# Mixture-of-experts block on one Trainium2 core: routing on tokens before their norm, and where the constants around it are prepared

## The chip, the cores and the metric

The kernel runs on one core of a Trainium2 chip. The metric is device time of one execution in microseconds (us), lower is better. A core has TensorE (PE: matrix products and transposes, in the order of its queue), VectorE (DVE), ScalarE (ACT), GpSimd (POOL), and SyncE (SP), which here only issues transfers. Each engine works through its own queue in order. An instruction that waits holds up all that stands behind it on its engine.

## The reference, cut to what matters

Two transformer blocks run one after the other. The change lies in the first, between the output projection of its mixers and its mixture of experts:

```python
x = layer_norm(DEEPNORM_ALPHA * x + mix @ w_out, ln1_g, ln1_b)   # 512 tokens x 1024
logits = x @ router_w + router_b                                 # 512 x 32 experts
top_val, top_idx = lax.top_k(logits, 4)
gate = softmax(top_val)
for e in range(32):                                              # rows = tokens that chose e
    hg, hl = split(x[rows] @ w_gu[e] + b_gu[e], 2)               # 1024 -> 2 x 1024
    hg, hl = min(hg, 7), clip(hl, -7, 7)
    y = ((hl + 1) * hg * sigmoid(1.702 * hg)) @ w_down[e] + b_down[e]
    ffn[rows] += gate * y
h = DEEPNORM_ALPHA * x + ffn
```

`layer_norm(x) = (x - mean) * rsqrt(var + 1e-5) * g + b`. All is float32. Since the experts' inputs depend on the top-4 choice, the logits are computed to float32 accuracy.

## The kernel before, in words

All of what follows is `block1_ffn` (from L1153). It handles the 512 tokens as 4 tiles of 128 (`NCH`), and three stretches of it matter here.

**Projection and router (393 to 470 us).** For each tile, two halves of 512 columns are projected into PSUM (bank `gu`). A product to float32 accuracy takes three matmuls with operands split in a high and a low part (`mm3`, L1148 to L1150), so a half is 24 matmuls. DVE adds the residual (L1283). `row_norm` takes statistics (DVE L1096, L1097, L1083), then a reciprocal root by Ln and Exp on ACT (L1084, L1085, each with its own table load), then normalises with two passes of 1024 columns on DVE (L1103, L1104). The normed tile is written to DRAM (`x1_d`, L1286; tiles 0 to 2 from POOL, tile 3 from SP). ACT makes a scaled copy (L1288), and POOL writes it to `h_d` (L1289), to which the experts' outputs are added later. PE transposes the normed tile in two halves of four (L1297), ACT copies each half out of PSUM (L1298), and 8 float32 matmuls against `rw` give the logits (L1301). DVE adds the bias (L1303), takes the top 4 and their softmax (L1311 to L1324).

After the last tile, small matmuls count each expert's tokens (L1331 to L1334), DVE forms ranks (L1335, L1336) and bfloat16 parts of the gates (`aux`, L1344 to L1348), and `slots` turns them into token lists: a comparison (L1408), four matmuls (L1411), and the index vector `ix` (L1419). POOL's indirect transfer gathers the first expert's 96 rows from `x1_d` with `ix` (L1428), and PE transposes them (L1230). **This gather is where the experts begin.**

**Constants, prepared beside the projection.** SP loads x, gains, biases and the expert bias `b_gu`. `bias` holds `b_gu` in three bfloat16 parts in three groups of 32 partitions: ACT rounds (L1260), and DVE takes differences and rounds them again, three subtractions and three casts of 32x2048 (L1265, L1266). The matmul L1443 adds that bias in the expert loop. The down bias `bdn` is loaded on ACT's queue and converted (L1354 to L1356).

**Experts (478 to 1690 us).** Each of 32 experts is 12 weight units of 1 MB. ACT rounds a unit to its high part `wh` (L1213), DVE subtracts it to get the low part `wl` (L1214), PE multiplies (L1148 to L1150). The units lie in a ring of 6 raw buffers and 3 spare ones, and 4 buffers for each part. For the first expert, unit 0 is used unsplit (L1451), and units 1 to 4 are split in pieces of 512 columns while the projection still runs; the low parts of units 1 and 2 are POOL's (8 pieces), those of 3 and 4 DVE's (8 pieces).

The program is written tile by tile; a scheduler builds each engine's queue from it, with its own estimate of when each instruction is ready. So code written later can stand earlier in a queue.

Of the kernel before, what the change touches and what calls it, by code (L numbers as in the profile page):

```python
# [126 lines left out]
def layout(inp):  # L127
# [34 lines left out]
    for n, k in (("w0", "rwkv_w0"), ("a0", "rwkv_a0"), ("k_k", "rwkv_k_k"), ("k_a", "rwkv_k_a"),  # L162
# [183 lines left out]
def bcast(ap_dram, off, n, parts=128):  # L346
    return bass.AP(tensor=ap_dram.tensor, offset=ap_dram.offset + off, ap=[[0, parts], [1, n]])
# [805 lines left out]
def block1_ffn(k, mix, wo, es_mix, b2):  # L1153
# [5 lines left out]
    with es:  # L1159
# [29 lines left out]
        def raw(n=2048, rows=128, p=ring, bufs=N_RAW):  # L1189
            return p.tile([128, 2048], F32, name="w", tag="w", bufs=bufs)[:rows, :n]  # L1190
# [47 lines left out]
        with tile_pool(tc, name="w1", bufs=1) as w1:  # L1238
# [9 lines left out]
            strict = w1.tile([128, 128], F32, name="strict")  # L1248
            nc.sync.dma_start(ident, A["cst"][:, 0:128])
            nc.sync.dma_start(strict, A["cst"][:, 128:256])  # L1250
            nc.sync.dma_start(cst2, A["cst"][:, CF["iota"][0]:CF["iota"][0] + 129])
            nc.sync.dma_start(rw, A["router_w"])
            nc.sync.dma_start(rb, bcast(A["router_b"], 0, 32))


            braw = raw(rows=96)
            for i in range(3):
                nc.sync.dma_start(braw[32 * i:32 * i + 32], A["b_gu"])
# [9 lines left out]
            ob_ = w1.tile([128, 128], BF, name="onesb")  # L1268
            V.tensor_copy(sb_, strict)
            G.memset(ob_, 1.0)  # L1270
            eye3 = sm.tile([128, 32], F32, name="eye3")
            V.tensor_add(eye3, ident[:, 0:32], ident[:, 32:64])
            V.tensor_add(eye3, eye3, ident[:, 64:96])
            M = w1.tile([128, NCH, N_EXP], F32, name="M")
            Mb = w1.tile([128, NCH, N_EXP], BF, name="Mb")
            for t in range(NCH):
                c = slice(128 * t, 128 * t + 128)
                for n in range(2):
# [58 lines left out]
            V.tensor_copy(cnt, p[:, NCH])  # L1337

            gr = w1.tile([128, NCH, N_EXP], F32, name="gr")
            V.tensor_copy(aux[:, :, :, 0].rearrange("p t e -> p (t e)"), pidx.to_broadcast([128, NCH * N_EXP]))  # L1340
            for t in range(NCH):
                G.memset(aux[:, t, :, 1], float(t))
            G.memset(aux[:, :, :, 2], 1.0)
            V.tensor_copy(aux[:, :, :, 3], Gm)  # L1344
            V.tensor_sub(gr, Gm, aux[:, :, :, 3])
            V.tensor_copy(aux[:, :, :, 4], gr)
            V.tensor_sub(gr, gr, aux[:, :, :, 4])
            V.tensor_copy(aux[:, :, :, 5], gr)  # L1348
            V.tensor_scalar(dslot, pidx, float(S), None, op0=OP.add)
# [45 lines left out]
        with tile_pool(tc, name="ex", bufs=1) as ex:  # L1395
# [106 lines left out]
            def expert_unit(e, i):  # L1502
# [1048 lines left out]
```

## Time and profile before

| | |
|---|---|
| median of 3 runs | 3124.77 us (3122.93 to 3128.39) |
| the profiled execution's own time | 3125.81 us |
| its span in the trace | 3124.0 us |
| mean granted TensorE clock | 0.964 of full speed |
| busy share over the span | PE 95%, DVE 65%, ACT 48%, POOL 17% |

The shares are averages over very different stages. The windows say what an engine does in one stretch, the timelines give the order within it, and "idle before <-releaser" says how long an engine waited and what ended the wait.

### The profile page before, as it was taken

The page shows a single profiled execution, that of the slowest core. Times are in us where ns is not written, and L with a number is a line of the kernel's source. Part 1 is how long each engine was busy: PE and PEld are TensorE (multiplying, and loading weights), DVE is VectorE, ACT ScalarE, POOL GpSimd, SP SyncE. Part 2 cuts the span into 40 slices and gives each one's busy share as a digit, 9 for nine tenths or more (in the row PEclk, how much of TensorE's full clock was granted, in tenths as well). Part 3 has the DMA queues.
Part 4 walks back from the last instruction along what each step waited for, and adds up shares of the span by engine and source line. Part 5 has one row for each costly group of instructions (what it writes and reads, how often), then busy time and mean ns, then how long its engine had stood idle before and what let it go on. Part 6 is the DMA issues. An engine that isn't in the chain of part 4 may idle for free. (4 is left out here: it accounts for less than half of the span.)

```text
span 3124.0 us, 41785 instructions
## 1 busy us (share of the span) xinstructions
PE 2966.2 (95%) x16609; PEld 2386.3 (76%) x16609; DVE 2037.0 (65%) x2862; ACT 1491.3 (48%) x1855; POOL 537.4 (17%) x444
## 2 busy tenths in 40 slices
PE   6899888999999999999999999999999899999997
PEld 4799765666666666666666888999999799888886
DVE  4755767988888888788887756654233846733324
ACT  4412346666666666666665633342222534432222
POOL 1210231101210000121002210320102501320104
PEclk8989989999999999999999989999999989999998
DMA  3201177989999999799996211122222211222221
GB/s 124 75 21 41 61 268 289 357 341 366 366 358 359 361 359 353 290 388 356 360 355 229 73 67 43 55 82 95 95 82 82 93 45 55 82 95 95 95 90 52
DMA packets 106263, 581.87 MB, mean 186 GB/s; under 512 B 13080, under 2 KB 13736, under 8 KB 56048
## 3 DMA queue, kind: packets, MB, share of 16 engines
q1 hardware_dynamic: 95120, 542.17, 44.9%
q0 software_dynamic: 10752, 36.47, 4.8%
q8 instruction: 132, 2.16, 0.3%
q10 hardware_dynamic: 192, 0.52, 0.1%
q14 instruction: 67, 0.55, 0.1%
HBM read 560.17 MB, written 18.94 MB: 185 GB/s over the span
## 5 line engine op out<-in xcount | busy, mean ns | idle before, releaser
L1214 DVE TENSOR_TENSOR wl<-w,wh 128x2048 fp32r<-128x2048 f32 (+1 forms) x367 | 800.8, 2197 | 125.7 <-ACT wh L1213 121.4
L1213 ACT ACTIVATE wh<-w 128x2048 fp32r<-128x2048 f32 (+1 forms) x375 | 668.3, 1810 | 51.4 <-PE gu L1150 34.9
L1816 PE MATMUL gu<-hh,w 128*128 128x264 f32 (+3 forms) x1336 | 419.0, 314 | 10.0 <-ACT hh L2518 10.0
L1817 PE MATMUL gu<-hl,w 128*128 128x264 f32 (+3 forms) x1336 | 415.6, 311 | 3.9 <-DVE hl L2520 3.8
L1818 PE MATMUL gu<-hh,w 128*128 128x264 f32 (+3 forms) x1336 | 413.5, 310 | 0.8 <-DVE w L1142 0.8
L1142 DVE TENSOR_TENSOR w<-w 128x1024 fp32r<-128x1024 f32 (+1 forms) x190 | 237.5, 1250 | 249.2 <-ACT w L1141 248.7
L1148 PE MATMUL gu<-wh,xT 128*96 128x512 f32 x896 | 371.9, 415 | 0.0
L1149 PE MATMUL gu<-wl,xT 128*96 128x512 f32 x896 | 359.4, 401 | 7.4 <-DVE wl L1214 7.2
L1150 PE MATMUL gu<-wh,xT 128*96 128x512 f32 x896 | 351.4, 392 | 0.0
L1141 ACT ACTIVATE w<-w 128x1024 fp32r<-128x1024 f32 (+1 forms) x194 | 201.3, 1038 | 297.7 <-PE gu L2338 89.6
L1816 PEld LDWEIGHTS gu<-hh,w 128*128 128x128 f32 x1336 | 260.0, 195 | 22.4 <-ACT hh L2518 11.6
L1817 PEld LDWEIGHTS gu<-hl,w 128*128 128x128 f32 x1336 | 260.0, 195 | 16.1 <-DVE hl L2520 5.0
L1818 PEld LDWEIGHTS gu<-hh,w 128*128 128x128 f32 x1336 | 260.5, 195 | 11.2 <-DVE w L1142 1.3
L1149 PE MATMUL py<-wl,hT 128*96 128x512 f32 x512 | 211.7, 413 | 1.8 <-DVE wl L1214 0.4
L1149 PEld LDWEIGHTS gu<-wl,xT 128*96 128x96 f32 x896 | 144.1, 161 | 87.1 <-DVE wl L1214 23.2
L1148 PE MATMUL py<-wh,hT 128*96 128x512 f32 x512 | 208.8, 408 | 1.4 <-ACT wh L1213 1.4
L1150 PE MATMUL py<-wh,hT 128*96 128x512 f32 x512 | 202.8, 399 | 0.0
L1148 PEld LDWEIGHTS gu<-wh,xT 128*96 128x96 f32 x896 | 144.4, 161 | 67.3 <-issue 7.4
L1150 PEld LDWEIGHTS gu<-wh,xT 128*96 128x96 f32 x896 | 145.4, 162 | 58.5
L2324 POOL TENSOR_TENSOR al<-fs,ah 128x528 fp32r<-128x528 f32 (+1 forms) x44 | 77.7, 1767 | 595.0 <-ACT ah L2323 595.0
L1428 POOL DMA_INDIRECT xg<-x_d,ix x32 | 72.8, 2275 | 505.5 <-DVE dx L1421 439.4
L1481 POOL DMA_INDIRECT h_d<-y,dx x31 | 60.6, 1955 | 526.2 <-ACT y L1480 496.6
(714 smaller groups left out, 6133.4 us busy)
## 6 DMA issues: line engine op xcount, KB each, us to landing
w<-in_wgu SPq DMA_DIRECT2D x256, 1024.0 KB, 8.4
w<-in_wdn SPq DMA_DIRECT2D x127, 1024.0 KB, 8.3
w<-in_w SPq DMA_DIRECT2D x88, 512.0 KB, 4.2
w<-in_w2f SPq DMA_DIRECT2D x43, 512.0 KB, 4.2
w<-in_w22a SPq DMA_DIRECT2D x32, 512.0 KB, 4.1
w<-in_w1f SPq DMA_DIRECT2D x18, 512.0 KB, 3.3
w<-in_w2o SPq DMA_DIRECT2D x16, 512.0 KB, 4.2
w<-in_w22b SPq DMA_DIRECT2D x16, 384.0 KB, 3.9
```

Of the source, the lines that this page charges most:

```text
L1141: nc.scalar.activation(h, w, AF.Copy)
L1142: (eng or nc.vector).tensor_sub(l, w, h.bitcast(F32))
L1148: PE.matmul(out, a[0], b[0], start=start, stop=False)
L1149: PE.matmul(out, a[0], b[1], start=False, stop=False)
L1150: PE.matmul(out, a[1], b[0], start=False, stop=stop)
L1213: ACT.activation(h[:, j], w[:, j], AF.Copy)
L1214: (early or V).tensor_sub(l[:, j], w[:, j], h[:, j].bitcast(F32))
L1428: gathers.append(G.indirect_dma_start(out=xg, out_offset=None, in_=x1_d, in_offset=bass.IndirectOffsetOnAxis(ap=ix[:, :1], axis=0)))
L1816: PE.matmul(p, w[0][:, kk], x[0][:, kk, c], start=kk == ks[0], stop=False)
L1817: PE.matmul(p, w[0][:, kk], x[1][:, kk, c], start=False, stop=False)
L1818: PE.matmul(p, w[1][:, kk], x[0][:, kk, c], start=False, stop=kk == ks[-1])
L2324: G.tensor_sub(a[1], ss[f], a[0].bitcast(F32))
```

## The change: what it does

1. Layer norm's gain is multiplied into the router's weights, and the logits are taken from tokens that are not yet normed: `logit = rs * (x @ (g*W) - mean * sum(g*W)) + (b @ W + router_b)`. The two sums over the weights come from 8 + 8 float32 matmuls with a matrix of ones, ahead of the first projection's end. The norm passes on DVE no longer stand ahead of the transposes.
2. The projection of tile t+1 is written ahead of the router of tile t.
3. The three-part expert bias is prepared by POOL (one +1 pass, a memset, two subtractions of 64 and 32 partitions x 2048) and ACT (three roundings), DVE no longer takes part. `b_gu` is loaded four times, not three.
4. All 16 low-part pieces of the first expert go to DVE; POOL did 8.
5. The gates' bfloat16 parts are taken per tile.
6. The down bias is loaded and converted in expert 2, in a raw buffer of the ring.
7. The scaled copy for `h_d` is made in place after `x1_d` has been written, and its code stands after the first gather's.
8. SP's loads are in another order: first tile, router and bias constants, gains, then tiles 1 to 3.

```diff
-            for t in range(NCH):
-                nc.sync.dma_start(x[:, t], A["x"][128 * t:128 * t + 128])
+            nc.sync.dma_start(x[:, 0], A["x"][0:128])
...
+            for t in range(1, NCH):
+                nc.sync.dma_start(x[:, t], A["x"][128 * t:128 * t + 128])
-            V.tensor_scalar(braw[:, 1024:], braw[:, 1024:], 1.0, None, op0=OP.add)
-            ACT.activation(bias[0:96], braw, AF.Copy)
-            G.memset(bias[96:128], 0.0)
-            for i in range(1, 3):
-                b_, w_ = bias[32 * i:32 * i + 32], braw[32 * i:32 * i + 32]
-                for _ in range(i):
-                    V.tensor_sub(w_, w_, b_)
-                    V.tensor_copy(b_, w_)
+            G.tensor_scalar(braw[:, 1024:], braw[:, 1024:], 1.0, None, op0=OP.add)
+            ACT.activation(bias, braw, AF.Copy)
+            G.memset(bias[32:64], 0.0)
+            for a in (64, 96):
+                G.tensor_sub(braw[a:128], braw[a:128], bias[a:128])
+                ACT.activation(bias[a:128], braw[a:128], AF.Copy)
...
+            V.tensor_mul(rwb, rw, gb[:, 1, :, None].to_broadcast([128, 8, 32]))
+            for j in range(8):
+                PE.matmul(p[:, 0], ones, rwb[:, j], start=j == 0, stop=j == 7)
+            V.tensor_add(rb, rb, p[:, 0])
+            V.tensor_mul(rw, rw, gb[:, 0, :, None].to_broadcast([128, 8, 32]))
+            for j in range(8):
+                PE.matmul(p[:, 1], ones, rw[:, j], start=j == 0, stop=j == 7)
+            V.tensor_scalar(nsg, p[:, 1], -1.0, None, op0=OP.mult)
...
+            def project(t):
...
                     V.scalar_tensor_tensor(xs, xs, ALPHA1, p, op0=OP.mult, op1=OP.add)
-                xt = x[:, t]
-                row_norm(k, w1, xt, xt, g1, b1, fast=True)
-                x1w = (nc.sync if t == NCH - 1 else nc.gpsimd).dma_start(x1_d[c], xt)
-                xa = w1.tile([128, 8, 128], F32, name="x1T", bufs=2).rearrange("p a b -> p (a b)")
-                ACT.activation(xa, xt, AF.Copy, scale=ALPHA1)
-                nc.gpsimd.dma_start(h_d[c], xa)
...
+                    V.bn_stats(st[:, n], xs)
+                V.bn_aggr(mv, st.rearrange("p a b -> p (a b)"))
+                return mv
+            mvs = [project(0)]
+            for t in range(NCH):
+                if t + 1 < NCH:
+                    mvs.append(project(t + 1))
...
                     ACT.activation(xT[:, 4 * n:4 * n + 4], p, AF.Copy)
+                fast_rsqrt(k, w1, mv[:, 1:2], rs, eps=1e-5)
                 p = bank("py", (128, N_EXP))
                 for j in range(8):
                     PE.matmul(p, xT[:, j], rw[:, j], start=j == 0, stop=j == 7)
+                V.scalar_tensor_tensor(xt, xt, mv[:, 0:1], g1, op0=OP.subtract, op1=OP.mult)
+                V.scalar_tensor_tensor(xt, xt, rs, b1, op0=OP.mult, op1=OP.add)
+                x1w = (nc.sync if t == NCH - 1 else nc.gpsimd).dma_start(x1_d[c], xt)
-                V.tensor_add(lg, p, rb)
+                V.scalar_tensor_tensor(lg, nsg, mv[:, 0:1], p, op0=OP.mult, op1=OP.add)
+                V.scalar_tensor_tensor(lg, lg, rs, rb, op0=OP.mult, op1=OP.add)
...
+                V.tensor_copy(aux[:, t, :, 3], Gm[:, t])
+                V.tensor_sub(gr[:, t], Gm[:, t], aux[:, t, :, 3])
...
-            V.tensor_copy(aux[:, :, :, 3], Gm)
-            V.tensor_sub(gr, Gm, aux[:, :, :, 3])
...
         def gates():
+            bd = raw(D)
             for i in range(4):
                 nc.scalar.dma_start(bd[32 * i:32 * i + 32], A["b_dn"])
             ACT.activation(bdn, bd, AF.Copy)
             V.tensor_sub(bdn[64:128], bd[64:128], bdn[64:128].bitcast(F32))
...
-                    return unit(src, early=(G if i < 3 else V if i < 5 else None) if e == 0 else None)
+                    return unit(src, early=V if e == 0 and i < 5 else None)
...
             st = rows(*sl[0])
+            for t in range(NCH):
+                ACT.activation(x[:, t], x[:, t], AF.Copy, scale=ALPHA1)
+                nc.gpsimd.dma_start(h_d[128 * t:128 * t + 128], x[:, t])
```

The new file has two lines more in its helpers and others further down, so its line numbers differ: `mm3` is L1150 to L1152, Ln and Exp L1086 and L1087, the low part L1216, the sums with ones L1285 and L1290, the residual L1311, the transposes L1326 and their copies L1327, the router's matmuls L1331, the norm passes L1332 and L1333, the `x1_d` write L1334, the bias parts L1264 to L1269, the scaled copy L1583 and its write L1584.

**ACT's queue, from tile 0's rsqrt to tile 1's transposed copies.** Before (tile 1):

```order
L1084 ACT_TABLE_LOAD
L1084 ACTIVATE rn_rs<-rn_rs 128x1
L1085 ACT_TABLE_LOAD
L1085 ACTIVATE rn_rs<-rn_rs 128x1
L1288 ACTIVATE x1T<-x 128x1024
L1298 ACTIVATE x1T<-tr 128x512
L1260 ACTIVATE bias<-w 96x2048
L1298 ACTIVATE x1T<-tr 128x512
```

Now (from tile 0's Exp to tile 1's copies):

```order
L1087 ACTIVATE rs<-rs 128x1
L1327 ACTIVATE x1T<-tr 128x512
L1265 ACTIVATE bias<-w 128x2048
L1327 ACTIVATE x1T<-tr 128x512
L1349 ACTIVATE gt<-gt 128x4
L1269 ACTIVATE bias<-w 64x2048
L1583 ACTIVATE x<-x 128x1024
L1269 ACTIVATE bias<-w 32x2048
L1086 ACT_TABLE_LOAD
L1086 ACTIVATE rs<-rs 128x1
L1087 ACT_TABLE_LOAD
L1087 ACTIVATE rs<-rs 128x1
L1327 ACTIVATE x1T<-tr 128x512 x2
```

The three roundings of the bias (`bias<-w`) now stand between tile 0's copies and tile 1's. Before, one stood there, between tile 1's copies, and DVE did the later two.

**POOL's queue over the same stretch.** Before, then now:

```order
L805 TENSOR_TENSOR wo_2851<-wraw,wo_2850 128x1024 x4
L1261 MEMSET bias 32x2048
L1270 MEMSET onesb 128x128
L1342 MEMSET aux 128x32 x4
L1343 MEMSET aux 128x128
L1397 MEMSET top 128x1
L1286 DMA x_d<-x 128x1024
L1289 DMA h_d<-x1T 128x1024
L1292 DMA h_d<-x 96x1024
```

```order
L807 TENSOR_TENSOR wo_2851<-wraw,wo_2850 128x1024 x4
L1274 MEMSET onesb 128x128
L1275 MEMSET ones 128x128
L1298 MEMSET aux 128x32 x4
L1299 MEMSET aux 128x128
L1424 MEMSET top 128x1
L1264 TENSOR_SCALAR w<-w 128x1024
L1266 MEMSET bias 32x2048
L1268 TENSOR_TENSOR w<-w,bias 64x2048
L1334 DMA x_d<-x 128x1024
L1268 TENSOR_TENSOR w<-w,bias 32x2048
L1584 DMA h_d<-x 128x1024
```

The +1 pass, the memset and both subtractions of the bias follow the setting-up of `aux`. The memset waits for ACT's first rounding, the second subtraction for ACT's second.

**PE's queue around tile 1's router, now** (`gu` is the projection, of tile 2 up to the first three rows and of tile 3 from the fifth on):

```order
L1150 MATMUL gu<-wo_2850,mix_2852 128x512
L1151 MATMUL gu<-wo_2851,mix_2852 128x512
L1152 MATMUL gu<-wo_2850,mix_2853 128x512
L1326 MATMUL tr<-fcst,x 128x128 x8
L1150 MATMUL gu<-wo_2848,mix_2852 128x512
L1331 MATMUL py<-rw,x1T 128x32 x4
L1151 MATMUL gu<-wo_2849,mix_2852 128x512
L1331 MATMUL py<-rw,x1T 128x32 x4
L1152 MATMUL gu<-wo_2848,mix_2853 128x512
```

Of tile 3's 48 matmuls one stands ahead of the router's first half, which needs ACT's copy `x1T`; the other 47 stand behind it.

**DVE's queue toward the index vector, now** (tile 3's last part; `wl` are first-expert pieces):

```order
L1216 TENSOR_TENSOR wl<-w,wh 128x512
L1358 TENSOR_REDUCE Gm<-oh 128x32
L1374 SCALAR_TENSOR_TENSOR Rm<-py,M 128x128
L1359 CAST aux<-Gm 128x32
L1376 COPY cnt<-py 128x32
L1360 TENSOR_TENSOR gr<-Gm,aux 128x32
L1375 TENSOR_SCALAR Rm<-Rm 128x128
L1361 CAST aux<-gr 128x32
L1216 TENSOR_TENSOR wl<-w,wh 128x512
L1362 TENSOR_TENSOR gr<-gr,aux 128x32
L1435 TENSOR_TENSOR o_3573<-fcst_2992,Rm 128x384
L1363 CAST aux<-gr 128x32
L1216 TENSOR_TENSOR wl<-w,wh 128x512
```

Before, no piece stood ahead of `ix`; now six do, these three and three earlier ones.

## Rows read from the trace of the kernel before

**Rows 1.** Groups of instructions, 478 to 1690 us (the experts): busy, mean ns | idle before, releasers.

```profile
L1213 ACT ACTIVATE wh<-w 128x2048 fp32r<-128x2048 f32 (+1 forms) x359 | 659.3, 1863 | 49.5 <-PE gu L1150 34.7 <-PE py L1150 6.0 <-ACT wh L1213 5.4
...
L1149 PE MATMUL gu<-wl,xT 128*96 128x512 f32 x896 | 359.4, 401 | 7.4 <-DVE wl L1214 7.2
```

**Rows 2.** Windows: us; busy (instructions) of PE, PEld, DVE, ACT, POOL; clock; DMA share; GB/s.

```profile
400.00:446.00 46.00, 45.42 (x224) 37.64 (x222) 31.62 (x65) 16.02 (x25) 8.31 (x16) 1.00 0.67 246
455.00:478.00 23.00, 7.26 (x47) 6.77 (x48) 19.64 (x52) 9.30 (x17) 10.33 (x8) 0.50 0.66 219
461.73:469.97 8.24, 1.08 (x11) 0.78 (x10) 6.86 (x32) 2.40 (x5) 0.00 (x0) 0.50 0.78 242
```

**Rows 3.** PE's timeline: start, duration, line, operation xcount [idle before <-releaser].

```profile
393.34 0.80 PE L1148 MATMUL gu<-wo,mix 128*128 128x512 f32 x1 [2.79 <-DVE mix L584]
...
398.57 0.40 PE L1148 MATMUL gu<-wo,mix 128*128 128x512 f32 x1
...
401.78 0.39 PE L1150 MATMUL gu<-wo,mix 128*128 128x512 f32 x1
...
413.35 1.03 PE L1297 MATMUL tr<-fcst,x 128*128 128x128 f32 x8
414.13 0.49 PE L1150 MATMUL gu<-wo,mix 128*128 128x512 f32 x1
...
414.93 0.97 PE L1301 MATMUL py<-rw,x1T 128*128 128x32 f32 x8
415.74 0.48 PE L1150 MATMUL gu<-wo,mix 128*128 128x512 f32 x1
...
425.66 1.07 PE L1297 MATMUL tr<-fcst,x 128*128 128x128 f32 x8 [0.57 <-DVE x L1104]
...
445.71 0.40 PE L1150 MATMUL gu<-wo,mix 128*128 128x512 f32 x1
...
477.20 1.51 PE L1230 MATMUL tr<-fcst,xg 96*128 96x96 f32 x8 [8.21 <-DMA xg<-x_d,ix]
```

**Rows 4.** DVE's timeline, 418 to 486 us.

```profile
420.60 0.69 DVE L1283 SCALAR_TENSOR_TENSOR x<-x,gu 128x512 f32<-128x512 f32 x1 [0.76 <-PE gu L1150]
...
437.66 2.28 DVE L1265 TENSOR_TENSOR w<-w,bias 32x2048 f32<-32x2048 f32 x1
...
445.96 1.28 DVE L1104 SCALAR_TENSOR_TENSOR x<-x,rn_rs,b 128x1024 f32<-128x1024 f32 x1
...
469.83 0.14 DVE L1419 CAST ix<-tk 96x1 int32<-96x1 f32 x1
...
470.02 2.48 DVE L1214 TENSOR_TENSOR wl<-w,wh 128x512 fp32r<-128x512 f32 x4
```

**Rows 5.** ACT's timeline, 418 to 456 us.

```profile
422.70 1.28 ACT L1085 ACT_TABLE_LOAD   x1
423.99 0.20 ACT L1085 ACTIVATE rn_rs<-rn_rs 128x1 f32<-128x1 f32 x1
...
426.58 0.58 ACT L1298 ACTIVATE x1T<-tr 128x512 f32<-128x512 f32 x1
427.05 1.90 ACT L1260 ACTIVATE bias<-w 96x2048 bf16<-96x2048 f32 x1
...
449.20 1.15 ACT L1213 ACTIVATE wh<-w 128x512 fp32r<-128x512 f32 x2
```

**Rows 6.** POOL's timeline, 390 to 480 us.

```profile
392.97 9.44 POOL L805 TENSOR_TENSOR wo<-wraw,wo 128x1024 fp32r<-128x1024 f32 x4 [35.92 <-ACT wo L804]
402.47 1.80 POOL L1261 MEMSET bias<- 32x2048 bf16 x1
...
449.18 10.67 POOL L1214 TENSOR_TENSOR wl<-w,wh 128x512 fp32r<-128x512 f32 x7
```

**Rows 7.** The `x1_d` writes from POOL (L1286): issue to landing.

```profile
DMA to landing us min/median/max: 2.9/7.1/8.6
```

**Rows 8.** The longest `h_d` write (L1292): issue to landing.

```profile
DMA to landing us min/median/max: 12.9/12.9/12.9
```

More of the change, by code (lines that the diff above doesn't have):

```diff
@@ L186, in layout @@
     o["router_w"] = np.ascontiguousarray(_pk(inp["router_w"][0]))
+    o["ln1c"] = np.ascontiguousarray(np.stack([inp[n][0].reshape(8, 128).T for n in ("ln1_g", "ln1_b")], 1))
     o["router_b"] = np.ascontiguousarray(inp["router_b"])
@@ L1243, in block1_ffn @@
             rb = w1.tile([128, 32], F32, name="rb")
-            for t in range(NCH):
-                nc.sync.dma_start(x[:, t], A["x"][128 * t:128 * t + 128])
+            gb = w1.tile([128, 2, 8], F32, name="gb")
+            nc.sync.dma_start(x[:, 0], A["x"][0:128])
+            strict = w1.tile([128, 128], F32, name="strict")
+            nc.sync.dma_start(ident, A["cst"][:, 0:128])
+            nc.sync.dma_start(rw, A["router_w"])
+            nc.sync.dma_start(gb, A["ln1c"])
+            nc.sync.dma_start(rb, bcast(A["router_b"], 0, 32))
@@ L1246, in block1_ffn @@
+            braw = raw(rows=128)
+            for i in range(4):
+                nc.sync.dma_start(braw[32 * i:32 * i + 32], A["b_gu"])
             nc.sync.dma_start(g1, bcast(A["rows2"], 0, D))
             nc.sync.dma_start(b1, bcast(A["rows2"], D, D))
-            strict = w1.tile([128, 128], F32, name="strict")
-            nc.sync.dma_start(ident, A["cst"][:, 0:128])
             nc.sync.dma_start(strict, A["cst"][:, 128:256])
             nc.sync.dma_start(cst2, A["cst"][:, CF["iota"][0]:CF["iota"][0] + 129])
-            nc.sync.dma_start(rw, A["router_w"])
@@ L1267, in block1_ffn @@
+            G.tensor_scalar(braw[:, 1024:], braw[:, 1024:], 1.0, None, op0=OP.add)
[4 more added lines that the diff above has]
+                ACT.activation(bias[a:128], braw[a:128], AF.Copy)
             sb_ = w1.tile([128, 128], BF, name="strictb")
             ob_ = w1.tile([128, 128], BF, name="onesb")
+            ones = w1.tile([128, 128], F32, name="ones")
@@ L1269, in block1_ffn @@
             V.tensor_copy(sb_, strict)
             G.memset(ob_, 1.0)
+            G.memset(ones, 1.0)
             eye3 = sm.tile([128, 32], F32, name="eye3")
-            V.tensor_add(eye3, ident[:, 0:32], ident[:, 32:64])
-            V.tensor_add(eye3, eye3, ident[:, 64:96])
+            V.tensor_add(eye3, ident[:, 0:32], ident[:, 64:96])
+            V.tensor_add(eye3, eye3, ident[:, 96:128])
+            rwb = w1.tile([128, 8, 128], F32, name="x1T", bufs=2)[:, :, 0:32]
+            V.tensor_mul(rwb, rw, gb[:, 1, :, None].to_broadcast([128, 8, 32]))
@@ L1274, in block1_ffn @@
             M = w1.tile([128, NCH, N_EXP], F32, name="M")
             Mb = w1.tile([128, NCH, N_EXP], BF, name="Mb")
+            gr = w1.tile([128, NCH, N_EXP], F32, name="gr")
+            V.tensor_copy(aux[:, :, :, 0].rearrange("p t e -> p (t e)"), pidx.to_broadcast([128, NCH * N_EXP]))
             for t in range(NCH):
+                G.memset(aux[:, t, :, 1], float(t))
+            G.memset(aux[:, :, :, 2], 1.0)
+            V.tensor_scalar(dslot, pidx, float(S), None, op0=OP.add)
+            def project(t):
@@ L1277, in block1_ffn @@
                 c = slice(128 * t, 128 * t + 128)
+                st = w1.tile([128, 2, 6], F32, name="st", bufs=2)
+                mv = w1.tile([128, 2], F32, name="mv", bufs=2)
                 for n in range(2):
@@ L1283, in block1_ffn @@
                     V.scalar_tensor_tensor(xs, xs, ALPHA1, p, op0=OP.mult, op1=OP.add)
-                xt = x[:, t]
-                row_norm(k, w1, xt, xt, g1, b1, fast=True)
-                x1w = (nc.sync if t == NCH - 1 else nc.gpsimd).dma_start(x1_d[c], xt)
-                xa = w1.tile([128, 8, 128], F32, name="x1T", bufs=2).rearrange("p a b -> p (a b)")
-                ACT.activation(xa, xt, AF.Copy, scale=ALPHA1)
-                nc.gpsimd.dma_start(h_d[c], xa)
-                if t == 0:
-                    nc.gpsimd.dma_start(h_d[S:], x[:NS, 0])
+                    V.bn_stats(st[:, n], xs)
[5 more added lines that the diff above has]
+                    mvs.append(project(t + 1))
+                c, xt, mv = slice(128 * t, 128 * t + 128), x[:, t], mvs[t]
+                rs = w1.tile([128, 1], F32, name="rs", bufs=2)
                 xT = w1.tile([128, 8, 128], F32, name="x1T", bufs=2)
-                for q in range(2):
+                for n in range(2):
                     p = bank("tr", (128, 4, 128))
                     for i in range(4):
-                        PE.transpose(p[:, i], xt[:, 512 * q + 128 * i:512 * q + 128 * i + 128], ident)
-                    ACT.activation(xT[:, 4 * q:4 * q + 4], p, AF.Copy)
+                        PE.transpose(p[:, i], xt[:, 512 * n + 128 * i:512 * n + 128 * i + 128], ident)
+                    ACT.activation(xT[:, 4 * n:4 * n + 4], p, AF.Copy)
+                fast_rsqrt(k, w1, mv[:, 1:2], rs, eps=1e-5)
                 p = bank("py", (128, N_EXP))
@@ L1337, in block1_ffn, with gates @@
             V.tensor_copy(cnt, p[:, NCH])
[L1339 to L1343, printed above, removed]
-            V.tensor_copy(aux[:, :, :, 3], Gm)
-            V.tensor_sub(gr, Gm, aux[:, :, :, 3])
[L1346 to L1349, printed above, removed]
             spare.append(es_b.enter_context(tile_pool(tc, name="spare2", bufs=1, side="right")))
             wb = es_b.enter_context(tile_pool(tc, name="wb", bufs=1, side="right"))
-            bd = w1.tile([128, 8, 128], F32, name="x1T", bufs=2).rearrange("p a b -> p (a b)")
+        def gates():
+            bd = raw(D)
             for i in range(4):
@@ L1553, in block1_ffn @@
             st = rows(*sl[0])
+            for t in range(NCH):
+                ACT.activation(x[:, t], x[:, t], AF.Copy, scale=ALPHA1)
+                nc.gpsimd.dma_start(h_d[128 * t:128 * t + 128], x[:, t])
+            nc.gpsimd.dma_start(h_d[S:], x[:NS, 0])
             sl.append(first(1))
```

10 lines of the change are left out of this document (5 added, 5 removed).

## The prediction

> **What bounds the kernel now.** I read four things in this order. First the groups of the experts' stretch: PE's low-part matmuls stood idle for 7.4 us in 1212 us, and ACT's splits waited mostly for PE [rows 1]. So PE sets the pace there, and a first gather that comes some us later moves the end by as much. Then the windows: from 400 to 446 us PE is busy 45.42 of 46.00 us at a granted clock of 1.00 (the 2.4 GHz level), while DVE, ACT and POOL have room; from 455 to 478 us PE is busy 7.26 of 23.00 at 0.50 (1.2 GHz) [rows 2]. So the projection is PE's, and after it comes a tail of small steps, most of them on DVE. Third PE's timeline, for prices and for the two fixed points: the last projection matmul starts at 445.71 and takes 0.23 until the next could start, so the projection ends at 445.94 [rows 3]. The index vector `ix` is ready at 469.83 + 0.14 = 469.97 [rows 4]. **The tail is 24.0 us.** Then PE waits for the gather [rows 3]. Last, the timelines of ACT and POOL, since the order of the changed program puts their bias work between two tiles.
>
> My sum is therefore the time of `ix` after the change against 469.97. All from there on is taken as shifted with it.
>
> **The projection, PE alone.** From 398.57 to 401.78 fourteen matmuls start, 0.229 each; elsewhere in the stretch 0.227, so I take 48 of a tile as 10.9 us [rows 3]. A tile's eight transposes hold the next start up by 0.78, and that matmul's successor by 0.10 more: 0.88. Half a router (4 steps, 8 passes) costs 0.81 + 0.10 = 0.91 the same way [rows 3]. The 16 float32 matmuls with ones have the shape of four such halves: 4 x 0.91 = 3.65, added to the projection. Two tiles' routers lay inside the projection before and do so now, so they cancel. The wait of 0.57 for the normed tile 1 goes, since transposes no longer need the norm [rows 3]. Without any new stall the projection would end at 445.94 + 3.65 - 0.57 = **449.0**.
>
> **The new stall.** ACT's queue now has the three bias roundings between tile 0's and tile 1's copies, and two of them wait for POOL's subtractions. In before, tile 1's second projected half reached DVE at 420.60, 0.1 after its end [rows 4]. Now tile 0's router (0.88 + 2 x 0.91 = 2.7) comes behind this point, and the ones (3.65) before it: 420.5 - 2.7 + 3.65 = 421.4. Four transposes and one copy (0.58) later, at 422.6, the chain starts:
> - ACT's first rounding, 1.90 by the one of before [rows 5]; POOL's memset behind it, 1.80 [rows 6];
> - subtraction, d; rounding 1.90; subtraction, d; rounding 1.90;
> - Ln and Exp of tile 1 with their table loads, 2 x (1.28 + 0.20) [rows 5]; the copy of half a tile, 0.58 [rows 5]; six hand-overs between engines, 0.1 each as in the 0.1 above.
>
> Without d that is 422.6 + 11.6 = 434.2. For d the trace has no row of this shape. POOL's four subtractions of 1024 columns took 9.44, so 2048 would take 4.7; its seven pieces of 512 beside a busy DVE took 10.67, so 2048 would take 6.1 [rows 6]. The number of partitions should not matter: on DVE 32 partitions x 2048 took 2.28 and four pieces of 128 x 512 took 2.48 [rows 4]. I take **d = 5.2**, nearer to the first, since DVE now has pauses; its lower bound is DVE's own 2.28. The chain ends at 444.6. PE is ready for tile 1's router after tile 2's projection (10.9), tile 0's transposes and router (2.7), tile 1's transposes (0.88) and one matmul (0.33): 421.4 + 14.8 = 436.2. **PE stands for 8.4 us**, with 47 matmuls of tile 3 behind it. The other engines' tile-3 work waits for those in turn.
>
> After the idle stretch at 393 us the first twelve matmuls took 5.23 (393.34 to 398.57) and not 2.7: the clock was at its lower level [rows 3]. I add 2.5 for the same after the stall; zero is the other bound. The projection then ends at 449.0 + 8.4 + 2.5 = **459.9**.
>
> POOL's rate itself: four passes of 1024 took 9.44, so 2.36 each, against half of 2.28 on DVE [rows 4, 6]. The Trainium skill, GPSIMD Engine Reference, section 3.1 on elementwise work, measures 4497 ns for a subtraction-like pass of 2048 float32 on GpSimd against 2293 ns on Vector and says to keep elementwise work on Vector; that speaks against this edit, and the trace agrees within 5% (4.7 for 2048). By its 4.5 for d the stall would be 7.0, and the sum below 1.4 us less.
>
> **The tail.** DVE has 62 operations from the last residual to `ix` in the new order. Two take 0.69 and four norm passes 1.28 [rows 4]: 6.5. Six are pieces of 0.62 (a quarter of 2.48) [rows 4]: 3.7; before, none stood ahead of `ix`. Fifty are small: 32 of their kind were busy 6.86 us [rows 2], less about 1.0 because five casts and differences of `aux` now have 32 columns and not 128, so 0.18 each: 9.2. Together 19.4. The last norm pass also waits for tile 3's Exp. By then ACT has done six pieces (0.57 each by 1.15 for two), four copies (0.53), two loads and two small steps, 8.5 [rows 5], and has waited some 1.8 for transposes at the lower clock, 10.3 in all. DVE is at that pass after 7.5, so it waits 2.8. Hand-overs 0.2. **Tail: 22.4**, 1.6 less than before: the norm left the way to the transposes, but the pieces came into it.
>
> `ix` is then ready at 459.9 + 22.4 = 482.3, 12.3 later. The profiled execution took 3125.81, which gives 3138.1. It is 1.04 above the median, so against the median the forecast is **3137.1 us**.
>
> **What I cost at nothing.** DVE's own bias work was under PE's projection, which never waited longer than the 0.57 for DVE [rows 2, 3]; taking it away gives nothing but that. POOL's +1 pass lies at 405 us, 17 us ahead of the chain; without that cover it would cost 2.4. The down bias in expert 2 takes one ring buffer and a wait of ACT under PE-bound work; 0 to 3 us. SP's new order lets weights start some 2 us later, all ahead of their use. The gates' parts are in the tail's count. The gather stands behind tile 3's `h_d` write on POOL, and that waits for tile 3's `x1_d` write to land and for ACT's scaling: 11.6 into the tail + 0.3 + 8.6 [rows 7] + 1.1 + 0.5 = 22.1, just under 22.4. With a landing of 12.9 [rows 8] it is 26.3, 3.9 late. These are the next two things to be late.
>
> **The rivals.** *Gather held by the write* (for it: the margin of 0.3; against: the median landing is 7.1 [rows 7]): 12.3 + 3.9 = +16.2, 3141.0; with d = 6.1 another 1.8, 3142.8. *POOL is quick, and the time stays* (the other side): the order alone causes no stall if each subtraction ends in time. PE stands 8.4 - 2 x (5.2 - d), so at DVE's 2.28 it stands 2.6, and no stall is left at d = 1.0. Then 449.0 + 22.4 gives +1.4, 3126.2. With 2.6 of stall but no loss of clock it is +4.0, 3128.8; it decides at d below about 2.1, where stall and clock together stay within +6.2. Against it: no POOL pass in the trace is that quick. *The tail is freed and the stall absent* (for it: pieces may fill waits that exist anyway, and matmuls with ones may run while PE waits for its weights): 445.4 + 15.9 (22.4 less 3.7 and 2.8) = 461.3, 8.7 earlier, 3116.1. Against it: PE was busy through the projection, and the pieces' places are fixed in DVE's queue. *The change not doing what it says* is excluded by the order.
>
> **How the numbers follow.** Stalled forecast 0.60 (with d from 4.7 to 6.1 and the tail's wait of 2.8 hidden or not: 3133 to 3139), gather held as well 0.12, no loss 0.18, gain 0.10. A measurement of this kernel can tell about 0.2%, 6.2 us, from no change. Slower by more is the first two, 0.72; same is the third and a fifth of the fourth, 0.20; faster 0.08. The range runs from 3126.0, the foot of the third, to 3143.0, the head of the second; it leaves out the fourth and an outlier above, under 0.2.
>
> **What would show it.** Right: PE idle some 8 us around 436 to 445 at the router's half of tile 1, released by ACT's copy; ACT there waiting twice for POOL's subtraction of about 5 us; a lower clock after it; `ix` near 482; no piece on POOL. Wrong: a POOL subtraction near 2 us; PE's projection unbroken until 449; or the gather released by something other than `ix`. If the experts' stretch from gather to end is longer or shorter by over 2 us, the shift does not pass to the end as taken.

## The result, and the profile after

The changed kernel takes 3143.38 us (median of 6 runs, 3134.23 to 3148.99) against 3123.85 (6 runs of before in the same sessions, 3112.45 to 3128.39). The ratio is 1.0072, with an interval from 1.0055 to 1.0090: **slower by 17 to 28 us**, where 12.3 was forecast. The profiled execution took 3148.99 us, span 3147.1, granted clock 0.962.

Totals scatter by up to 20 us (29 runs of before: 3110.6 to 3130.9), and part of that arises ahead of the stretch studied here: in the profiles the projection starts between 379.2 and 395.4 us, though the experiments' edits concern only what comes behind. So the mechanisms are read from stretches that begin at the projection's start. There kernels with the same order agree: the tail is 20.4 us in four of them (changed, e2, e3, f0), and the projection 53.2 or 53.3 in four of the five with the same three repairs, 54.1 in the fifth. From there to the end the kernel before took 2730.7 us (3124.0 - 393.3) and the changed one 2754.8 (3147.1 - 392.3): 24.1 more.

That starting point flatters the kernel before by 3.1 us. There PE waited 2.79 us for the last mixer's output before the projection [rows 3]; in the changed kernel, and in all its variants, the projection follows that mixer's matmuls with no wait, 1.60 us after their start and not 4.73. Counted from those matmuls (388.61 before, 390.73 after) the change costs 21.0 us. Which of its eight parts removed the wait was not tested.

```profile
388.61 1.94 PE L580 MATMUL ps<-cst,ml_h 128*128 128x128 f32 x8 [4.32 <-DVE ml_h L572]
```

| stretch, us | before | forecast | after |
|---|---|---|---|
| projection, first to last matmul | 52.6 | 66.6 | 75.1 |
| tail, to the index vector `ix` | 24.0 | 22.4 | 20.4 |
| `ix` to the transposes of the gathered rows | 7.2 | 7.2 | 10.4 |
| sum | 83.9 | 96.2 | 105.9 |

PE's timeline after the change, with the waits that answer to [rows 3]:

```profile
390.73 1.94 PE L582 MATMUL ps<-cst,ml_h 128*128 128x128 f32 x8 [4.32 <-DVE ml_h L574]
392.33 0.78 PE L1150 MATMUL gu<-wo,mix 128*128 128x512 f32 x1
...
404.60 0.50 PE L1151 MATMUL gu<-wo,mix 128*128 128x512 f32 x1 [0.68 <-POOL wo L807]
...
408.09 3.59 PE L1285 MATMUL py<-x1T,ones 128*128 128x32 f32 x16 [2.76 <-DVE x1T L1282]
411.49 0.77 PE L1150 MATMUL gu<-wo,mix 128*128 128x512 f32 x1
...
412.49 3.46 PE L1290 MATMUL py<-rw,ones 128*128 128x32 f32 x16
415.76 0.77 PE L1152 MATMUL gu<-wo,mix 128*128 128x512 f32 x1
...
451.23 1.92 PE L1331 MATMUL py<-rw,x1T 128*128 128x32 f32 x8 [6.49 <-ACT x1T L1327]
452.96 0.77 PE L1151 MATMUL gu<-wo,mix 128*128 128x512 f32 x1
...
467.44 1.03 PE L1326 MATMUL tr<-fcst,x 128*128 128x128 f32 x8
...
498.22 1.52 PE L1232 MATMUL tr<-fcst,xg 96*128 96x96 f32 x8 [11.41 <-DMA xg<-x_d,ix]
```

Two places broke the projection. The forecast one is there: PE waits 6.49 us for ACT's `x1T` at tile 1's router. The other is at the matmuls with ones (L1285, L1290): a wait of 2.76, then 3.40 and 3.27 us for what was costed at 1.8 each, and matmuls that start 0.43 apart, not 0.23. Two windows give the clock (the columns are those of [rows 2]); before, it was 1.00 from 400 to 446 us [rows 2]:

```profile
411.00:422.00 11.00, 11.00 (x38) 9.50 (x38) 2.12 (x6) 1.69 (x3) 0.00 (x0) 0.53 0.98 406
452.00:462.00 10.00, 10.00 (x38) 8.54 (x38) 4.93 (x21) 3.81 (x6) 1.07 (x2) 0.65 0.44 179
```

Who held PE at the ones stands in three queues, DVE's, ACT's and POOL's:

```profile
406.01 0.15 DVE L1426 TENSOR_SCALAR top<-top 128x1 f32<-128x1 f32 x1 [10.61 <-ACT top L1425]
406.10 0.69 DVE L1311 SCALAR_TENSOR_TENSOR x<-x,gu 128x512 f32<-128x512 f32 x1
...
407.53 0.42 DVE L1282 TENSOR_TENSOR x1T<-rw,gb 128x256 f32<-128x256 f32 x1
```

```profile
405.78 0.20 ACT L1425 ACTIVATE top<-top 128x1 f32<-128x1 f32 x1 [6.61 <-POOL top L1424]
```

```profile
402.18 2.37 POOL L807 TENSOR_TENSOR wo<-wraw,wo 128x1024 fp32r<-128x1024 f32 x1
...
405.42 0.31 POOL L1424 MEMSET top<- 128x1 f32 x1
```

The weights' product with the bias (L1282) stands in DVE's queue behind a step on the constant `top`. That step waits for ACT's sigmoid, the sigmoid for POOL's memset of `top`, and the memset stands behind POOL's last pass over the output weights (L807, to 404.5) and its setting-up of other constants. A constant that nobody needs before the experts held up PE.

The stall at tile 1, in ACT's and POOL's queues:

```profile
430.73 1.90 ACT L1265 ACTIVATE bias<-w 128x2048 bf16<-128x2048 f32 x1
...
439.40 0.21 ACT L1349 ACTIVATE gt<-gt 128x4 f32<-128x4 f32 x1 [6.28 <-DVE gt L1348]
439.63 1.91 ACT L1269 ACTIVATE bias<-w 64x2048 bf16<-64x2048 f32 x1
...
445.76 1.91 ACT L1269 ACTIVATE bias<-w 32x2048 bf16<-32x2048 f32 x1 [3.12 <-POOL w L1268]
447.68 1.28 ACT L1086 ACT_TABLE_LOAD   x1
...
450.60 1.06 ACT L1327 ACTIVATE x1T<-tr 128x512 f32<-128x512 f32 x2
```

```profile
432.69 1.80 POOL L1266 MEMSET bias<- 32x2048 bf16 x1 [24.41 <-ACT bias L1265]
434.56 4.10 POOL L1268 TENSOR_TENSOR w<-w,bias 64x2048 f32<-64x2048 f32 x1
...
441.63 4.09 POOL L1268 TENSOR_TENSOR w<-w,bias 32x2048 f32<-32x2048 f32 x1 [2.42 <-ACT bias L1269]
```

The chain runs as forecast, rounding, memset, subtraction, rounding, subtraction, rounding, two table loads, copy. Only d is 4.1, not 5.2. DVE beside it shows something that was not forecast:

```profile
435.25 3.46 DVE L1337 SCALAR_TENSOR_TENSOR lg<-lg,rs,rb 128x32 f32<-128x32 f32 x1
...
441.80 4.07 DVE L1353 TENSOR_TENSOR oh<-fcst,ixf 128x128 f32<-128x128 f32 x1
```

Two small steps take 3.46 and 4.07 us and end 0.05 and 0.15 us after POOL's two subtractions. The first of them enters the chain: ACT's second rounding stands behind the exponential of tile 0's gates (L1349), whose operand DVE makes after that step. So the rounding starts 0.97 us after POOL's subtraction has ended (438.66), where the forecast has 0.1.

### The profile page after: what moved, and what is told of

Same layout as the page of the kernel before. It is cut to its first block, busy times and chain, and to the rows that moved or that the text cites. A ratio compares the mean times of both kernels' runs of the same rounds, so it can differ in the third digit from the quotient of the medians.

```text
span 3147.1 us, 41865 instructions
## 1 busy us (share of the span) xinstructions
PE 2977.9 (95%) x16641; PEld 2395.5 (76%) x16641; DVE 2032.7 (65%) x2886; ACT 1494.3 (47%) x1857; POOL 543.5 (17%) x440
## 5 line engine op out<-in xcount | busy, mean ns | idle before, releaser
L1216 DVE TENSOR_TENSOR wl<-w,wh 128x2048 fp32r<-128x2048 f32 (+1 forms) x375 | 805.8, 2163 | 122.2 <-ACT wh L1215 119.8
L1150 PE MATMUL gu<-wh,xT 128*96 128x512 f32 x896 | 371.9, 415 | 0.0
L1152 PE MATMUL gu<-wh,xT 128*96 128x512 f32 x896 | 351.4, 392 | 0.0
L1150 PE MATMUL py<-wh,hT 128*96 128x512 f32 x512 | 209.9, 410 | 1.4 <-ACT wh L1215 1.4
L1151 PEld LDWEIGHTS gu<-wl,xT 128*96 128x96 f32 x896 | 144.1, 161 | 87.4 <-DVE wl L1216 23.4
L1152 PE MATMUL py<-wh,hT 128*96 128x512 f32 x512 | 203.7, 400 | 0.0
L1150 PEld LDWEIGHTS gu<-wh,xT 128*96 128x96 f32 x896 | 144.4, 161 | 67.6 <-issue 7.5
L1152 PEld LDWEIGHTS gu<-wh,xT 128*96 128x96 f32 x896 | 145.4, 162 | 58.4
```

The lines of the kernel that those rows point to most:

```text
L1150: PE.matmul(out, a[0], b[0], start=start, stop=False)
L1151: PE.matmul(out, a[0], b[1], start=False, stop=False)
L1152: PE.matmul(out, a[1], b[0], start=False, stop=stop)
L1216: (early or V).tensor_sub(l[:, j], w[:, j], h[:, j].bitcast(F32))
```

## The experiments

Theory S is the forecast's stall. Theory O came from the trace after: the sums with ones. The numbers in the table are us of the profiled execution, from the projection's start as above; the ratio is that of the whole times to before, with its 95% interval.

| kernel | projection | tail | `ix` to transposes | sum | ratio |
|---|---|---|---|---|---|
| before | 52.6 | 24.0 | 7.2 | 83.9 | 1 |
| changed | 75.1 | 20.4 | 10.4 | 105.9 | 1.0072 (1.0055 to 1.0090) |
| e1 | 63.5 | 28.3 | 10.2 | 102.0 | 1.0072 (1.0046 to 1.0098) |
| e2 | 68.6 | 20.4 | 9.9 | 98.9 | 1.0049 (1.0026 to 1.0071) |
| e12 | 57.2 | 28.4 | 10.7 | 96.3 | 1.0032 (1.0012 to 1.0051) |
| e3 | 65.1 | 20.4 | 10.5 | 95.9 | 1.0039 (1.0016 to 1.0062) |
| f0 | 59.0 | 20.4 | 10.0 | 89.4 | 1.0009 (0.9990 to 1.0028) |
| e23r | 53.2 | 22.1 | 10.9 | 86.2 | 1.0020 (1.0001 to 1.0039) |
| e23rg | 54.1 | 23.6 | 6.4 | 84.0 | 1.0026 (1.0008 to 1.0044) |
| e23rgb | 53.3 | 22.0 | 5.3 | 80.6 | 1.0019 (1.0003 to 1.0036) |
| f1 | 53.2 | 20.9 | 10.7 | 84.9 | 1.0005 (0.9989 to 1.0020) |
| f2 | 53.2 | 21.2 | 12.8 | 87.2 | 1.0011 (0.9995 to 1.0027) |
| gp | 73.5 | 23.4 | 9.9 | 106.7 | 1.0081 (1.0052 to 1.0110) |

**e1, the bias chain first.** ACT's copies for tile 0, its Ln and Exp for tiles 0 and 1 and the first scaled copy are ordered behind the last rounding, POOL's first `x1_d` write behind the last subtraction:

```diff
...
-                ACT.activation(bias[a:128], braw[a:128], AF.Copy)
+                rnd = ACT.activation(bias[a:128], braw[a:128], AF.Copy)
...
+                    with tc.issue_after(rnd.ins) if t == 0 else nullcontext():
                         ACT.activation(xT[:, 4 * n:4 * n + 4], p, AF.Copy)
+                with tc.issue_after(rnd.ins) if t < 2 else nullcontext():
                     fast_rsqrt(k, w1, mv[:, 1:2], rs, eps=1e-5)
...
```

> The changed kernel with one order edit: ACT's three roundings and POOL's two subtractions of the expert bias are held ahead of tile 0's transposed copies, Ln and Exp; nothing is computed otherwise. Theory S (the bias chain between tile 0's and tile 1's copies is most of the loss): the wait of 6.5 us of PE at tile 1's router is gone, and with it about 3.3 us at the lower clock, so the kernel gains 10 us on the changed one and stands about 10 us above before. Theory O (the sums with ones are most of the loss): the wait goes, but the time stays within 3 us of the changed kernel, since PE loses its clock at the ones anyway.

The stall was gone and the projection 11.7 us shorter, but the tail grew by 7.9, and the total did not move (ratio 1.0072 again). In ACT's queue tile 0's Exp now stood behind tile 1's first copy, and tile 1's Ln and Exp behind that. So tile 1's norm was late against the projection: its `x1_d` write was issued 5.3 us before the projection's end (442.76 of 448.03), in the changed kernel 10.4. The scaled copy of tile 1, which waits for that write, stood in ACT's queue ahead of tile 2's work, and PE waited for it:

```profile
449.83 1.06 ACT L1587 ACTIVATE x<-x 128x1024 f32<-128x1024 f32 x1 [4.09 <-DMA x_d<-x]
...
454.34 1.06 ACT L1328 ACTIVATE x1T<-tr 128x512 f32<-128x512 f32 x2
```

```profile
454.97 1.91 PE L1333 MATMUL py<-rw,x1T 128*128 128x32 f32 x8 [5.69 <-ACT x1T L1328]
```

A clean test of S it is not: a wait that is ordered away in one queue came back behind it.

**e2, the weights ahead of `top`.** DVE's step on `top` is ordered behind the second product:

```diff
+            with tc.issue_after(rwg.ins):
                 V.tensor_scalar(top, top, 7.0, None, op0=OP.mult)
```

> The changed kernel with one order edit: DVE multiplies the router's weights by bias and gain ahead of its step on the constant top, which waits for ACT's sigmoid and POOL's memset. Theory O: the sums with ones no longer wait 2.8 us, and about 6 us of lower clock behind that wait go too; 9 us less than the changed kernel, some 11 above before. Theory S: the stall at tile 1 comes that much earlier or grows, since its chain starts from tile 0's copies; under 3 us are gained.

The wait was gone, the projection 6.5 us shorter and the sum of the table 7.0, not 9. The rest of O stayed, and a window shows what it is:

```profile
403.00:406.00 3.00, 3.00 (x23) 2.75 (x23) 0.77 (x3) 2.00 (x5) 3.00 (x7) 0.94 1.05 405
406.00:412.00 6.00, 6.00 (x22) 5.32 (x23) 1.94 (x5) 0.50 (x2) 0.44 (x1) 0.50 1.03 421
```

```profile
403.31 1.86 PE L1285 MATMUL py<-x1T,ones 128*128 128x32 f32 x16
...
405.56 3.42 PE L1290 MATMUL py<-rw,ones 128*128 128x32 f32 x16
408.79 0.77 PE L1152 MATMUL gu<-wo,mix 128*128 128x512 f32 x1
```

The second eight (L1290) take 3.42 where the first took 1.86, and the clock is at 0.50 while PE is busy 6.00 of 6.00 us. PE had not waited for them: what it did before the clock fell were 32-column matmuls, the first eight. Shortly before those it had waited twice for POOL's output weights, 0.56 and 0.68 us. Two such waits (0.65 and 0.67) stand at the same place in f1 below, where one matmul replaces the sixteen, and there the clock stays at 1.00:

```profile
401.00:414.00 13.00, 12.84 (x65) 10.57 (x64) 1.99 (x8) 4.46 (x8) 2.10 (x1) 1.00 1.02 419
```

**e12, both orders.**

> Both order edits together. If S and O are separate losses on one path, 10 + 9 us are gained on the changed kernel: from 2 us below before to 4 above it, with PE unbroken from 393 to some 449 us but for short waits on POOL's output weights. If something else bounds it (the gather, the tail of DVE), it stays 8 us or more above before.

It gained 17.9 in the projection, but kept e1's longer tail: 9.6 in all, and not the 19 of separate losses. The tail's 8.0 is most of that miss; the sum stands 12.4 above before, which is the other branch of the expectation.

**e3, subtractions on DVE.** The scheduler then also puts tile 1's Ln and Exp behind its copies, so that the chain is shorter by these 3.0 us as well, beside 2 x (4.1 - 2.3) = 3.6 by the subtractions. So e3 tests the chain as a whole and not POOL's rate alone: either part by itself is shorter than the wait of 6.49.

```diff
-                G.tensor_sub(braw[a:128], braw[a:128], bias[a:128])
+                V.tensor_sub(braw[a:128], braw[a:128], bias[a:128])
```

> The changed kernel with the two bias subtractions on DVE in place of POOL, in the order that the scheduler then gives. Theory S: the subtractions take 2.3 in place of 4.1 us, and the stall at tile 1 shrinks from 6.5 to under 2 us; 7 to 10 us less than the changed kernel. DVE's two small steps of 3.5 and 4.1 us beside POOL's subtractions are short again if POOL's use of memory caused them. Theory O: within 3 us of the changed kernel.

As S expected: no wait at tile 1's router, 10.0 us off the projection, the tail unchanged at 20.4. DVE's two small steps are short:

```profile
444.48 0.23 DVE L1337 SCALAR_TENSOR_TENSOR lg<-lg,rs,rb 128x32 f32<-128x32 f32 x1
...
448.37 0.28 DVE L1353 TENSOR_TENSOR oh<-fcst,ixf 128x128 f32<-128x128 f32 x1
```

**f0, e2 and e3 together.**

> The changed kernel with the subtractions on DVE and the router's weights ahead of top, the sixteen matmuls with ones left as they are. If S and O add up, the projection takes 75.1 - 10.0 - 6.5 = 58.5 us, and what the run with reduced sums had below that (53.2) is the sixteen matmuls themselves: 5.3 us, not the 3.65 of the forecast. If it takes 56 or 57, the two losses overlap (a shared stretch at the lower clock), and the matmuls cost their 3.65.

59.0 against 58.5: S and O add up, but for 0.5.

**e23r, the sums reduced first.** DVE adds the 8 blocks, and one matmul with 64 columns takes the place of sixteen:

```diff
-            for j in range(8):
-                PE.matmul(p[:, 0], ones, rwb[:, j], start=j == 0, stop=j == 7)
+            V.tensor_reduce(s2[:, 0], rwb.rearrange("p a b -> p b a"), AX.X, OP.add)
...
+            PE.matmul(p, ones, s2, start=True, stop=True)
```

> Three repairs on the changed kernel: subtractions on DVE, the router's weights ahead of top, and DVE adds each weight product over its 8 blocks first, so that one float32 matmul with ones takes the place of sixteen. If S, O and the matmuls' own 3.6 us are three separate losses of the projection, it takes 75.1 - 10.0 - 6.5 - 3.3 = 55 us (52.6 before), and from the projection's start to the transposes of the first gathered rows there are 86 us (105.9 in the changed kernel, 83.9 before). If the ones cost only what they wait for, some 89.

53.2, and not 55: the sixteen matmuls cost 5.8 by themselves (59.0 - 53.2), and so O is 6.5 + 5.8 = 12.3 us, more than S. The projection is now within 0.6 of before's.

**e23rg, the gather first.** POOL writes one column behind the gather, DVE reads it, and the pieces of units 2 to 4 stand behind that read:

```diff
+            with tc.issue_after(gathers[0].ins):
+                G.memset(gd[:, 0:1], 0.0)
+            gv = V.tensor_copy(gd[:, 1:2], gd[:, 0:1])
...
+                    with tc.issue_after(gv.ins) if e == 0 and 1 < i < 5 else nullcontext():
```

> As the run before it in this list, and DVE's pieces of units 2 to 4 wait until POOL has issued the first gather (a one-column memset on POOL behind the gather, read by DVE ahead of the pieces). Theory H (POOL's gather waits for memory while DVE's pieces run back to back): the gather's issue takes 0.9 in place of 6.1 us, the rows come 5 us sooner, and two pieces fewer ahead of the index vector give 1.2 more: 79 to 80 us from the projection's start to the transposes. Rival: the issue takes 6.1 us because the first gather always does, and nothing but the 1.2 is gained: 84 to 85.

H holds for the gather: its issue took 0.98. In the changed kernel it took 6.12, beside nine pieces on DVE:

```profile
487.87 5.49 DVE L1216 TENSOR_TENSOR wl<-w,wh 128x512 fp32r<-128x512 f32 x9
```

```profile
488.11 6.12 POOL L1455 DMA_INDIRECT xg<-x_d,ix  x1 [3.10 <-DVE ix L1446]
```

The sum is 84.0, not 79 to 80, since this tail was 1.5 longer than in e23r and the projection 0.9, where PE waited 1.09 for the sums' operand. That 84.0 is the rival's number is chance: the issue time decides. And the gain did not last, as the next run shows.

**e23rgb, the down bias early.** Its five lines go back from `gates` to their place in the kernel before:

```diff
         def gates():
-            bd = raw(D)
-            for i in range(4):
-                nc.scalar.dma_start(bd[32 * i:32 * i + 32], A["b_dn"])
...
```

> As the run before it in this list, and the down bias is loaded and converted where the kernel before did it, ahead of the experts. Theory B (the move into expert 2 costs 4 us there, by waits of PE for POOL's copies of the gates and a lower clock behind them): the stretch from the first gather's transposes to the gather for expert 4 is 4 us shorter than in the run before, as long as before's 148, and the total is 3 to 8 us below before. Rival: the wait there is the gates' own, and the stretch does not change; the total is then within 4 us of before.

The 148 in that text mixes the two traces and is void; the fifth and sixth gather can be compared instead. They stand 40.0 us apart before, 43.5 in the changed kernel, 42.6 in e23rg and 40.0 here and in f1. So the edit gave 2.5 there and 1.0 more up to the seventh gather, and B holds for 3.5 us. From the fifth to the seventh the changed kernel lost 4.2 in all (3.5 and 0.7). The lost time in it lies here (before, one wait of 1.50):

```profile
607.01 0.33 PE L1392 MATMUL tr<-fcst,g 128*128 128x128 f32 x1 [0.92 <-POOL g L1391]
...
608.73 0.33 PE L1392 MATMUL tr<-fcst,g 128*128 128x128 f32 x1 [0.94 <-POOL g L1391]
...
611.05 0.47 PE L1392 MATMUL tr<-fcst,g 128*128 128x128 f32 x1 [1.27 <-POOL g L1391]
```

These waits are 1.6 us longer than before's, and the clock fell with them; the first window is the changed kernel's, the second before's:

```profile
605.00:612.00 7.00, 3.87 (x17) 2.07 (x16) 5.78 (x4) 3.34 (x4) 4.41 (x3) 0.79 0.90 343
```

```profile
585.00:590.00 5.00, 3.91 (x16) 1.58 (x14) 4.84 (x3) 2.29 (x2) 2.46 (x3) 1.00 1.02 426
```

The total is 1 to 11 us above before, not below it. The second gather took the first one's gain back:

```profile
454.79 0.98 POOL L1456 DMA_INDIRECT xg<-x_d,ix  x1 [3.22 <-DVE ix L1447]
...
465.28 3.19 POOL L1456 DMA_INDIRECT xg<-x_d,ix  x1 [9.39 <-DVE wl L1216]
```

```profile
459.80 1.51 PE L1232 MATMUL tr<-fcst,xg 96*128 96x96 f32 x8 [6.28 <-DMA xg<-x_d,ix]
...
476.17 1.51 PE L1232 MATMUL tr<-fcst,xg 96*128 96x96 f32 x8 [7.05 <-DMA xg<-x_d,ix]
```

PE waits 7.05 us for the second expert's rows (before, it did not wait for them). That gather runs beside five postponed pieces on DVE (3.08 us from 464.56) and takes 3.19 to issue. By the third gather's issue this run stands 103.0 us from the projection's start, and f1, which postpones no piece, 99.1, though f1's first rows came 4.3 later.

**gp, pieces back on POOL.**

```diff
-                    return unit(src, early=V if e == 0 and i < 5 else None)
+                    return unit(src, early=(G if i < 3 else V if i < 5 else None) if e == 0 else None)
```

> The changed kernel with the 8 low parts of units 1 and 2 back on POOL. Theory of the forecast: the tail from the projection's end to the index vector loses 3 pieces or more on DVE, up to 3.7 us, but gets POOL's work beside DVE's small steps, which took 3.1 us more beside it in before: tail 19 to 22 (20.4 in the changed kernel). By theory H the gather's issue is shorter, 1 to 4 us, since fewer pieces stand behind the index vector.

The tail got 3.0 longer, above the expected range: POOL's pieces stretch DVE's norm passes (2.30 in place of 1.28 for one). The gather's issue is 2.51, as H expects.

**f1, all repairs but the wait for the gather.**

> Subtractions on DVE, weights ahead of top, sums reduced on DVE first, down bias converted early as before; DVE's pieces as in the changed kernel, with no wait for the gather. From the projection's start to the first gathered rows' transposes 86 us (83.9 before); the two lost microseconds come back by the end of the experts only if expert 2 is as quick as before and the first two gathers cost 3 to 4 us. Total from 2 us below to 4 us above before.

84.9, and 2730.5 us from the projection's start to the end (before: 2730.7). Totals agree as well: 3121.79 against 3121.88. From the last mixer's matmuls f1 takes 3.3 us less than before; the totals, whose interval is 5 us wide to either side, do not show it.

**f2, unit 2 unsplit.**

```diff
-                if i == 0:
+                if i == 0 or u == 2:
                     return (load(src),)
```

> As f1, and unit 2 of the first expert is multiplied unsplit, as unit 0 is, so that 4 of DVE's 16 pieces and ACT's 4 fall away, for some 1 us more on PE. By theory H the gather is held by 6 pieces behind the index vector, not 9: its issue takes 4 to 5 us, the rows come 1.5 us sooner, and the second gather as well; 1 to 3 us below f1. If DVE does not bound this stretch, the same as f1 or 1 us above it.

A miss: the gather's issue is 6.51. DVE had six pieces behind `ix`, as expected, but with no pause behind them came a whole unit's low part in one step of 128x2048, 2.28 us. The row merges both:

```profile
465.08 5.89 DVE L1216 TENSOR_TENSOR wl<-w,wh 128x512 fp32r<-128x512 f32 x7
```

```profile
465.32 6.51 POOL L1456 DMA_INDIRECT xg<-x_d,ix  x1 [3.91 <-DVE dx L1449]
```

What counts is how long DVE runs without a pause behind `ix`, not how many pieces there are. No version beat before by more than the measurement tells; f1 cannot be told from it.

## Why the prediction was right and wrong

**Right:** the direction and its mechanism. The stall is in the queues where it was placed, in time some 8 us later, and cost 10.0 us (e3) where 8.4 + 2.5 = 10.9 was forecast. That the sum came so near is partly luck: d was 4.1, below the 4.7 to 6.1 that it was taken from, so the wait was 6.49 and not 8.4, but the lower clock behind it cost some 3.5 (10.0 - 6.5) and not 2.5. No rival of the other side came about: POOL's subtraction was not quick, and the gather was not held by the `h_d` write, which POOL issued at 484.48, before `ix` at 487.82.

**Wrong, the size:** 19.5 at the medians, 21.0 from the last mixer's matmuls and 24.1 from the projection's start, where 12.3 was given; the range's head was 3143.0, the median 3143.38. Three steps failed.

- *"The 16 float32 matmuls with ones have the shape of four such halves: 4 x 0.91 = 3.65."* They cost 12.3: 6.5 by the wait behind `top` and the clock that went with it (e2), 5.8 by themselves (f0 against e23r): the 3.65 as costed, and a lower clock that they brought on (the windows of e2). The prediction priced the matmuls, and never asked what their operands wait for in DVE's queue. The rival that hid them under PE's idle time had the sign wrong.
- *"All from there on is taken as shifted with it."* The gather's issue took 6.12, not 3.11, because nine pieces and not four stand behind `ix`: 3.2 us. The prediction took the pieces' place ahead of `ix` into the tail, and what they do to the gather behind it at nothing. Its own sign of this, over 2 us more between gather and end, came about: 5.3 us from `ix` to the end.
- *"The down bias in expert 2 ... 0 to 3 us."* It was 4.2 (3.5 and 0.7), costed at zero; 3.5 of it went with the early conversion (e23rg against e23rgb).

The tail was 2.0 better than forecast: DVE's wait for tile 3's Exp was 2.81 as worked out, and the small steps were cheaper. The sum: 22.5 for the projection, -3.6 for the tail, 7.9 from `ix` to the last gather (4.06 up to the third gather, 3.17 of them at the first; 4.15 at the down bias; -0.32 elsewhere), and -2.6 behind the last gather, where the 13 profiles lie between 1544.4 and 1551.3 us with no edit there: 24.2, against 24.1. The 3.1 us that the change gained ahead of the projection are in no term of the prediction, which kept before's wait of 2.79 as it was; they made the miss smaller.

## What to carry to other kernels

An instruction added to the bounding engine is priced with its operands' queues: walk back from each operand through the engine that makes it, and ask what stands ahead there. Where a scheduler sets the issue order, name what waits behind the longest step of an engine that is mostly idle: here a constant on POOL held up ACT, DVE and then PE. Before work is moved off a busy engine, ask whether the engine it goes to is a link in a chain that the bounding engine waits for; here POOL was.

## What the runs showed of the hardware

**POOL's gather waits for the end of DVE's run.** In four kernels the gather's issue ended 0.86 or 0.87 us after the last of DVE's uninterrupted pieces: before at 473.37 (DVE to 472.50), after at 494.23 (493.36), gp at 479.05 (478.19), f2 at 471.83 (470.97). A short pause is enough: before, DVE's next step began 0.04 us after the pieces, and the gather ended beside it. With DVE idle it took 0.98 (e23rg). The Trainium skill, SBUF — State Buffer, section "Who interferes with whom", says that a DVE instruction with two SBUF inputs contends with GpSimd's reads, and infers that descriptor generation does not suffer from it. This gather reads its indices from SBUF, and it did wait, through nine DVE instructions and not one; whether the indices are the reason was not tested.

**It goes both ways.** DVE's two small steps above ended with POOL's subtractions (3.46 and 4.07 us against 0.23 and 0.28 in e3). By the Trainium skill, SBUF — State Buffer, section "SBUF: two separate sides", of a DVE instruction with two SBUF inputs and a GpSimd one that reads SBUF, whichever starts first keeps the shared ports for its whole instruction. These rows agree: POOL's subtractions had started 0.69 and 0.17 us earlier.

**The clock fell behind small matmuls while PE was busy throughout:** 0.50 with PE busy 6.00 of 6.00 us (e2), and 1.00 where one matmul stood for the sixteen (f1, 401 to 414 us).
